# Residual rows of both mixers' ends formed by two row instructions instead of eight channel pieces turned back

## The chip, the cores and the metric

The kernel runs on one core of one Trainium2 chip. The metric is the device time of one execution, in microseconds (us). The engines that compute are TensorE (PE; its weight loads are listed apart as PEld), VectorE (DVE), ScalarE (ACT) and GpSimd (POOL); SyncE (SP) issues most of the DMAs.

## The reference, cut to what matters

The program is a trunk of two layers over 256 context tokens and 512 latent tokens of width 1024. Each layer is a sequence mixer (a linear recurrence, LRU, in layer 0; RWKV in layer 1), then a layer norm, then a mixture of 64 experts with 8 chosen for each token and one shared expert. What the change touches is what stands between mixer and experts:

```python
h = _layer_norm(DEEPNORM_ALPHA * h + m[2] * y, post_ln_g[i, 0], post_ln_b[i, 0])
u = _modulate(h, m[3], m[4])            # u = h * (1 + m[4]) + m[3]
y = _moe_ffn(u, router, bias, w_gu, w_down, sh_gu, sh_down)
h = _layer_norm(DEEPNORM_ALPHA * h + m[5] * y, post_ln_g[i, 1], post_ln_b[i, 1])
```

So each token needs two things at the end of a mixer: `u`, which the router and the experts read, and `h`, the residual, which is read again only behind the experts. Layer 0 has all 768 tokens here (6 tiles of 128), layer 1 only the 512 latent ones (4 tiles).

## The kernel before, in words

The stages follow one another: LRU mixer (to about 340 us), its end (340 to 478), the choice of experts, the sort and the experts of layer 0 (to about 1400), RWKV mixer (to about 2500), its end (to 2581), the experts of layer 1 (to about 3345) and the last norm. Products in fp32 are made from pieces split in two, three matmuls each. Inside the experts' loops the order of instructions is written by hand; everywhere else, the mixers' ends among it, a list scheduler of the compiler orders them, and each engine then runs its own list in that order.

A mixer's end is driven by `outputs` (L423). For each tile `t` it runs `gemm(t)`, the mixer's output product, and steps a generator `res(t, ...)` of `mixer_res` (L1911) from `yield` to `yield`, so that the steps of neighbouring tiles lie between each other. The steps of one tile:

- load the residual row tile `hin` (3 buffers in layer 0, 4 in layer 1); `post_ln` or `norm` (L400 to L421) leaves in it the normed rows, without the norm's gain and bias;
- turn it: eight 128x128 transposes on PE put the tile with channels on the partitions into `rt_px` (L1955). `rt_px` is 4 KB per partition in PSUM and has one buffer; whoever wants it next waits until its readers are done;
- form `uT`, the experts' input with channels on the partitions: eight pieces, each one instruction with a scale and a bias per channel (`mbc`, in which gain and modulation are folded together). Pieces with k in `UD` (1, 3, 5, 7) go to DVE (L1962), the others to ACT (L1964);
- form `hT`, the finished residual with channels on the partitions, in the same way with `mbx`: odd pieces on ACT (L1969), even ones on DVE (L1971);
- `route` (L685 to L717): eight matmuls of `uT` with the router's weights into `rt_pr`, a tanh on ACT (L687), and some twenty small DVE instructions; L712 writes `Mt`, the chosen experts, L717 `Wt`, their weights;
- turn `uT` back into rows (eight transposes into `rt_px`, L1977, and two copies on ACT, L1979) and send the rows to DRAM as `u_d` (L1984, on SP);
- turn `hT` back in the same way (again `rt_px`, again L1977 and L1979) and send the rows as `hm_d` (L1987, on POOL).

So `rt_px` is filled three times for a tile. When the last tile's product has been issued, the shared expert's weights are loaded into the mixer's freed memory (`ew`), split on ACT, DVE and POOL, and some of the shared expert's matmuls (`ph`, `py`, L95) are put among the steps of the tiles. When every tile's `Mt` is there, the sort begins on PE with `cc` (L793); the experts' weight loads follow behind it.

Of the kernel before, what the change touches and what calls it, by code (L numbers as in the profile page):

```python
# [9 lines left out]
F32 = mybir.dt.float32  # L10
# [3 lines left out]
AF = mybir.ActivationFunctionType  # L14
OP = mybir.AluOpType
# [4 lines left out]
D = 1024  # L20
KD = D // 128
# [6 lines left out]
NE = 64  # L28
# [243 lines left out]
class Kern:  # L272
# [181 lines left out]
    def lru(self, before, prepare, res, early):  # L454
        nc, ins, tc = self.nc, self.ins, self.tc
        with ExitStack() as st:
# [88 lines left out]

            S = {}

            def p0(j):
# [13 lines left out]
                for s, t0, n in SEGS:  # L562
# [3 lines left out]
                    for a in range(1, 4):  # L566
                        nc.vector.scalar_tensor_tensor(x, z[:, o + a:o + a + n], cw[:, a, j:j + 1], x, op0=OP.mult, op1=OP.add)
                S[j] = {"xc": xc}

# [187 lines left out]
    def moe(self, i, T, caps, u_d, acc_d, C, early, wst, late):  # L757
# [4 lines left out]
        nc, ins, tc = self.nc, self.ins, self.tc  # L762
# [3 lines left out]
        with ExitStack() as st:  # L766
            cq = st.enter_context(self.pool(name=f"moe_c{i}", bufs=1))
            wk = st.enter_context(self.pool(name=f"moe_k{i}", bufs=2))
# [12 lines left out]
            elist, ov, nov, novi = row("elist", 64, I32, 1), row("ov", 64, F32, 1), row("nov", 1, F32, 1), row("novi", 1, I32, 1)  # L781
# [190 lines left out]
            with tc.manual_schedule():  # L972
# [19 lines left out]
                for n in range(NB + 2):  # L992
# [40 lines left out]
                    elif n >= 2:  # L1033
                        nc.gpsimd.indirect_dma_start(out=acc_d[n % 2], out_offset=bass.IndirectOffsetOnAxis(ap=ix, axis=0),  # L1034
                                                     in_=yt[:C], in_offset=None, compute_op=OP.add)
                    if n == NB - 1:
                        late(lambda t, s: E.wp.tile(s, F32, name=f"late_{t}", tag=t, bufs=E.BW[t]))


            nr = nc.values_load(novi[0:1, 0:1], min_val=0, max_val=NE)  # L1040
            with tc.For_i(0, nr, 1) as it:
                e = nc.sync.value_load(olist[0:1, 1, bass.ds(it, 1)], min_val=0, max_val=NE - 1)
                p = nc.vector.value_load(olist[0:1, 0, bass.ds(it, 1)], min_val=0, max_val=NE - 1)
# [832 lines left out]
ES = ((2, 4, 2, 4), (2, 1, 4, 1))  # L1876
HB = (3, 4)
UB = (3, 4)
UD = ((1, 3, 5, 7), (1, 3, 5, 7))
VB = 5  # L1880
BUF = {'X1': 2, 'X2': 2, 'NN': 4, 'no': 2, 'ZT': 8, 'SU': 2, 'O': 2}

# [8 lines left out]
def trunk(tc, ins, out):  # L1891
    K = Kern(tc, ins, out)
    nc = tc.nc

    with ExitStack() as st:
# [12 lines left out]
        def stream(i, t):  # L1908
            return CTX if i == 0 and t < 2 else LAT

        def mixer_res(i):  # L1911
            P = {}

            def prepare(pool, psr):
                S = (CTX, LAT) if i == 0 else (LAT,)
                if i:
                    P["z1"] = K.ln_params(pool, 0, 1)
                for s in S:
                    if i == 0:
                        P[2, s] = pool.tile([128, D], F32, name=f"mb{s}")  # L1920
                        K.bcast_row(P[2, s], i, s, 2)

                    r = pool.tile([4 * KD, 128], F32, name=f"mbr{s}")
                    for n, x in enumerate((ins["post_ln_g"][i, 0], ins["post_ln_b"][i, 0], K.m_d[i][s, 4 * D:5 * D], K.m_d[i][s, 3 * D:4 * D])):
                        K.load(r[n * KD:(n + 1) * KD], x.rearrange("(k p) -> k p", p=128))
                    ps = psr.tile([128, 4, KD], F32, name="mb_ps", tag="rt_pr")
                    nc.tensor.transpose(ps.rearrange("p n k -> p (n k)"), r, K.ident[:4 * KD, :4 * KD])
                    x = pool.tile([128, 4, KD], F32, name=f"mbx{s}")
                    nc.vector.tensor_copy(x, ps)
                    P["x", s] = x  # L1930
                    c = P["c", s] = pool.tile([128, 2, KD], F32, name=f"mbc{s}")
                    nc.vector.scalar_tensor_tensor(c[:, 0], x[:, 2], 1.0, x[:, 0], op0=OP.add, op1=OP.mult)
                    nc.vector.scalar_tensor_tensor(c[:, 1], x[:, 2], 1.0, x[:, 1], op0=OP.add, op1=OP.mult)
                    nc.vector.tensor_tensor(c[:, 1], c[:, 1], x[:, 3], op=OP.add)

            def res(t, ys, wk, psr):
                s = stream(i, t)
                h = wk.tile([128, D], F32, name="hin", bufs=HB[i])
# [14 lines left out]
                px = psr.tile([128, KD, 128], F32, name="rt_px")  # L1953
# [6 lines left out]
                for k in range(KD):  # L1960
                    if k in UD[i]:
                        nc.vector.tensor_scalar(uT[:, k], px[:, k], c[:, 0, k:k + 1], c[:, 1, k:k + 1], op0=OP.mult, op1=OP.add)  # L1962
                    else:
                        nc.scalar.activation(uT[:, k], px[:, k], AF.Identity, scale=c[:, 0, k:k + 1], bias=c[:, 1, k:k + 1])  # L1964
                x = P["x", s]
                hT = wk.tile([128, KD, 128], F32, name="rt_hT", bufs=1)
                for k in range(KD):
                    if k % 2:
                        nc.scalar.activation(hT[:, k], px[:, k], AF.Identity, scale=x[:, 0, k:k + 1], bias=x[:, 1, k:k + 1])  # L1969
                    else:  # L1970
                        nc.vector.tensor_scalar(hT[:, k], px[:, k], x[:, 0, k:k + 1], x[:, 1, k:k + 1], op0=OP.mult, op1=OP.add)  # L1971

                def back(xT, y):

                    px = psr.tile([128, KD, 128], F32, name="rt_px")
                    for k in range(KD):
                        nc.tensor.transpose(px[:, k, :], xT[:, k], K.ident)  # L1977
                    for k in range(0, KD, 4):
                        nc.scalar.activation(y[:, k * 128:k * 128 + 512].rearrange("p (k d) -> p k d", k=4), px[:, k:k + 4, :], AF.Copy)  # L1979
# [3 lines left out]
                back(uT, u)  # L1983
                nc.sync.dma_start(u_d[i][t * 128:(t + 1) * 128, :], u)  # L1984
                yield
                back(hT, h)
                nc.gpsimd.dma_start(hm_d[i][t * 128:(t + 1) * 128, :], h)  # L1987
            return prepare, res

# [70 lines left out]
        fs, f = right()  # L2060
# [17 lines left out]
        P = {}  # L2078
        K.rwkv(first, done, begin, res)
        with P["rs"]:  # L2080
# [3 lines left out]
            with wst:  # L2084
                fs, f = right()
# [49 lines left out]
```

## Time and profile before

| what | time |
|---|---|
| median of 3 runs (3382.0 to 3406.42) | 3397.05 us |
| profiled execution | 3397.3 us |
| its span in the trace | 3395.5 us |
| PE busy in the span | 2976.2 us (88%) |
| DVE busy | 2403.6 us (71%) |
| ACT busy | 2006.7 us (59%) |
| POOL busy | 1125.8 us (33%) |
| mean granted TensorE clock, share of full speed | 0.878 |

An execution is one core's, so the time is that of this core. Busy shares over the whole span mix stages with different limits; the rows below are taken from the stretches that the change touches. A line of a timeline is one instruction, or several alike in a row ("x8"): its start, its time, the engine, the source line, what it writes and reads, and in brackets how long the engine stood idle before it and what ended that.

### The profile page before, as it was taken

Reading aid. Unit: us, or ns where it says so; the run is one execution under the profiler, and the core shown is the slowest. Engines: PE = TensorE matmul, PEld = TensorE weight load, DVE = VectorE, ACT = ScalarE, POOL = GpSimd, SP = SyncE. Lnnn points to the kernel's source line nnn. Section 1 sums busy time; section 2 is a strip of 40 time slices with the busy share of each in tenths; the row PEclk is TensorE's granted clock in tenths of the full one; section 3 lists DMA queues with packets and bytes.
Section 4 is the critical chain, followed back from the end, with each engine's and each line's share of the span. In section 5 each row is a group of like instructions: output and inputs, shape, how many; then the busy total and the mean of one; then the engine's idle time right before and its main releaser. Section 6 shows DMA issues by size and latency. Waiting matters only on the chain. (4 is left out here: it accounts for less than half of the span.)

```text
span 3395.5 us, 52648 instructions
## 1 busy us (share of the span) xinstructions
PE 2976.2 (88%) x17929; PEld 2076.3 (61%) x17929; DVE 2403.6 (71%) x4728; ACT 2006.7 (59%) x3835; POOL 1125.8 (33%) x1341
## 2 busy tenths in 40 slices
PE   7998768899999998498989998999877898899993
PEld 3665756667676665376757776767655665555551
DVE  4555557788878887767774756765554888789886
ACT  2664335667766776666645454654333676677773
POOL 0323002333333433122544455543421232333331
PEclk9998879999999999699975678577977999899997
DMA  6446339999999998433675666566524999999995
GB/s 218 126 133 195 116 147 271 307 318 333 339 292 322 330 314 283 137 105 125 152 192 147 176 186 184 147 185 169 171 97 172 320 327 330 309 353 356 344 341 175
DMA packets 329665, 784.71 MB, mean 231 GB/s; under 512 B 129176, under 2 KB 194008, under 8 KB 279856
## 3 DMA queue, kind: packets, MB, share of 16 engines
q1 hardware_dynamic: 276576, 668.36, 59.5%
q0 software_dynamic: 52816, 112.93, 13.9%
q8 instruction: 145, 2.38, 0.3%
q14 instruction: 128, 1.05, 0.1%
HBM read 644.66 MB, written 134.82 MB: 230 GB/s over the span
## 5 line engine op out<-in xcount | busy, mean ns | idle before, releaser
L95 PE MATMUL ph<-w1s,xs 128*128 128x512 f32 (+21 forms) x3216 | 808.1, 401 | 5.6 <-ACT xs L305 2.7
L308 DVE TENSOR_TENSOR w1s<-w,w1s 128x1024 fp32r<-128x1024 f32 x516 | 609.1, 1221 | 67.5 <-ACT w1s L305 66.7
L95 PEld LDWEIGHTS ph<-w1s,xs 128*128 128x128 f32 (+21 forms) x3216 | 490.6, 157 | 247.3 <-DVE xs L308 13.1
L1034 POOL DMA_INDIRECT acc_d<-yt,ix x150 | 303.9, 2026 | 949.3 <-ACT yt L141 312.5
L305 ACT ACTIVATE w1s<-w 128x1024 fp32r<-128x1024 f32 x516 | 516.8, 1057 | 5.3 <-DMA w<-in_moe_w_gu_dram 4.9
L95 PE MATMUL py<-w2s,hT 128*128 128x512 f32 (+22 forms) x1608 | 428.6, 417 | 38.4 <-DVE yt L138 25.5
L95 PEld LDWEIGHTS py<-w2s,hT 128*128 128x128 f32 (+22 forms) x1608 | 250.5, 163 | 160.4 <-issue 34.1
L305 ACT ACTIVATE xs<-px 128x512 fp32r<-128x512 f32 (+23 forms) x287 | 131.2, 457 | 358.8 <-DVE xs L308 224.8
L308 DVE TENSOR_TENSOR w2s<-w,w2s 128x1024 fp32r<-128x1024 f32 x258 | 303.6, 1217 | 8.1 <-ACT w2s L305 8.1
L305 ACT ACTIVATE w2s<-w 128x1024 fp32r<-128x1024 f32 x258 | 258.3, 1053 | 13.2 <-DMA w<-in_moe_w_down_dram 13.1
L308 DVE TENSOR_TENSOR xs<-px,xs 128x512 fp32r<-128x512 f32 (+23 forms) x287 | 146.4, 510 | 157.3 <-ACT xs L305 157.3
L932 POOL DMA_INDIRECT xg<-u_d,ix x150 | 215.8, 1438 | 89.1 <-issue 42.2
L141 ACT ACTIVATE yt<-py 128x512 f32<-128x512 f32 (+20 forms) x282 | 151.6, 593 | 45.6 <-PE py L95 25.7
L73 PE MATMUL px<-ident,xg 128*128 128x128 f32 (+25 forms) x1224 | 129.6, 249 | 44.8 <-DMA xg<-u_d,ix 44.8
L73 PEld LDWEIGHTS px<-ident,xg 128*128 128x128 f32 (+25 forms) x1224 | 111.2, 144 | 68.8 <-issue 61.0
L1690 POOL TENSOR_TENSOR SU<-SU,pC 64x128 f32<-64x128 f32 x176 | 96.6, 554 | 154.2 <-DVE SU L1710 130.9
L542 PE MATMUL in_ps<-uT,w_in 128*128 128x256 f32 (+1 forms) x768 | 143.3, 344 | 4.1 <-ACT w_in L305 2.1
L1189 PE MATMUL pt_ps<-xm,rw 128*128 128x256 f32 (+1 forms) x600 | 130.0, 370 | 14.3 <-ACT xm L305 7.9
L542 PEld LDWEIGHTS in_ps<-uT,w_in 128*128 128x128 f32 x768 | 118.6, 189 | 35.1 <-ACT w_in L305 6.4
L1535 PE MATMUL sc_ps<-X,uBK 64*128 64x128 f32 (+1 forms) x768 | 133.6, 358 | 0.7 <-POOL upt L1494 0.6
L1189 PEld LDWEIGHTS pt_ps<-xm,rw 128*128 128x128 f32 x600 | 102.1, 192 | 45.4 <-ACT xm L305 9.2
L1535 PEld LDWEIGHTS sc_ps<-X,uBK 64*128 64x128 f32 x768 | 113.3, 253 | 21.1 <-issue 8.4
(461 smaller groups left out, 5578.0 us busy)
## 6 DMA issues: line engine op xcount, KB each, us to landing
w<-in_moe_w_gu_dram SPq DMA_DIRECT2D x256, 1024.0 KB
w<-in_moe_w_down_dram SPq DMA_DIRECT2D x128, 1024.0 KB
ada_w<-in_ada_w_dram SPq DMA_DIRECT2D x96, 512.0 KB
O<-op SPq DMA_DIRECT2D x32, 768.0 KB
op<-NN SPq DMA_DIRECT2D x48, 256.0 KB
op<-NN SPq DMA_DIRECT2D x32, 384.0 KB
SU<-v_d SPq DMA_DIRECT2D x48, 256.0 KB
acc_d<-zrow SPq DMA_DIRECT2D x17, 512.0 KB
```

Of the source, the lines that this page charges most:

```text
L73: self.nc.tensor.transpose(px[:, k, :C], x[:C, k * 128:(k + 1) * 128], self.K.ident[:C, :C])
L95: self.nc.tensor.matmul(out[:C], x[a][:, :C], w[b], start=(first and a + b == 0), stop=(last and a == 1))
L141: self.nc.scalar.activation(yt[:C, c * 512:(c + 1) * 512], py[:C, c, :], AF.Copy)
L305: nc.scalar.activation(hi, src, AF.Copy)
L308: (lo_eng or nc.vector).tensor_tensor(lo, src, hi.bitcast(F32), op=OP.subtract)
L542: nc.tensor.matmul(ps[:, s, :n], whl[a][:, k, :], uT[b][:, k, t0:t0 + n], start=(k == 0 and a == 0 and b == 0), stop=(k == KD - 1 and a == 1))
L932: nc.gpsimd.indirect_dma_start(out=x[:C], out_offset=None, in_=u_d, in_offset=bass.IndirectOffsetOnAxis(ap=IW[blk][0], axis=0))
L1034: nc.gpsimd.indirect_dma_start(out=acc_d[n % 2], out_offset=bass.IndirectOffsetOnAxis(ap=ix, axis=0), in_=yt[:C], in_offset=None, compute_ ...
L1189: nc.tensor.matmul(ps[:, s, :n], w[a][:, k, :], x[k][b][:, s0:s0 + n], start=(k == 0 and a == 0 and b == 0), stop=(k == KD - 1 and a == 1))
L1535: nc.tensor.matmul(sc[h][:, c, :nr, :], BK[r64(h), c].rearrange("p a t -> p (a t)"), X[r64(h), :, c, :], start=True, stop=True)
L1690: nc.gpsimd.tensor_tensor(SV[z, g2][r64(0), :, k2], S[r64(0), :, k], P[z, g]["pC"][:, k].to_broadcast([64, 2, 64]), op=OP.mult)
```

## The change

Four things are changed, all but the last in `mixer_res`:

- The eight `hT` pieces, the eight transposes that turn them back and the two ACT copies behind these are gone. In their place two DVE instructions multiply the row tile `hin` by the gain and add the bias, in place and over all 1024 channels at once; they stand behind the sending of `u_d`. `hm_d` is sent as before.
- For that `prepare` loads two more tiles per mixer, the rows `post_ln_g` and `post_ln_b` spread over 128 partitions (512 KB each). In layer 1, the corresponding rows of the experts' norm of layer 0 get names of their own.
- `UD` is empty: all eight `uT` pieces are made on ACT.
- In the experts' function, the load of the number of overflow blocks (`nr`) into the engines' registers is moved from behind the hand-ordered part to its last step, ahead of the `late` tiles.

```diff
@@ -1034,10 +1034,10 @@
                     if n == NB - 1:
+                        nr = nc.values_load(novi[0:1, 0:1], min_val=0, max_val=NE)
                         late(lambda t, s: E.wp.tile(s, F32, name=f"late_{t}", tag=t, bufs=E.BW[t]))
 
 
-            nr = nc.values_load(novi[0:1, 0:1], min_val=0, max_val=NE)
             with tc.For_i(0, nr, 1) as it:
@@ -1876,7 +1876,7 @@
-UD = ((1, 3, 5, 7), (1, 3, 5, 7))
+UD = ((), ())
@@ -1913,8 +1913,13 @@
             def prepare(pool, psr):
                 S = (CTX, LAT) if i == 0 else (LAT,)
+                P["ln"] = K.ln_params(pool, i, 0)
                 if i:
-                    P["z1"] = K.ln_params(pool, 0, 1)
+                    P["z1"] = []
+                    for n in ("post_ln_g", "post_ln_b"):
+                        x = pool.tile([128, D], F32, name=f"z1_{n}")
+                        K.load(x, ins[n][0, 1:2, :].to_broadcast([128, D]))
+                        P["z1"].append(x)
@@ -1927,7 +1932,6 @@
-                    P["x", s] = x
@@ -1962,14 +1966,6 @@
-                x = P["x", s]
-                hT = wk.tile([128, KD, 128], F32, name="rt_hT", bufs=1)
-                for k in range(KD):
-                    if k % 2:
-                        nc.scalar.activation(hT[:, k], px[:, k], AF.Identity, scale=x[:, 0, k:k + 1], bias=x[:, 1, k:k + 1])
-                    else:
-                        nc.vector.tensor_scalar(hT[:, k], px[:, k], x[:, 0, k:k + 1], x[:, 1, k:k + 1], op0=OP.mult, op1=OP.add)
@@ -1983,7 +1979,8 @@
                 back(uT, u)
                 nc.sync.dma_start(u_d[i][t * 128:(t + 1) * 128, :], u)
                 yield
-                back(hT, h)
+                for x, op in zip(P["ln"], (OP.mult, OP.add)):
+                    nc.vector.tensor_tensor(h, h, x, op=op)
                 nc.gpsimd.dma_start(hm_d[i][t * 128:(t + 1) * 128, :], h)
```

The scheduler makes new lists from this. Three places of them are shown, by the program's order alone. First PE at the end of the RWKV mixer, from the end of the last product (L1863) on; before:

```order
L1863 MATMUL ro_ps<-hin,alpha_i 128x512 x2
L1977 MATMUL rt_px<-ident,rt_uT 128x128 x8
L1977 MATMUL rt_px<-ident,rt_hT 128x128 x8
L1955 MATMUL rt_px<-ident,hin 128x128 x8
L95 MATMUL ph<-ew_26112,xs_26210 128x512
```

and in the changed kernel (L1959 and L1973 are L1955 and L1977 of before; `ph` is the shared expert):

```order
L1863 MATMUL ro_ps<-hin,alpha_i 128x512 x2
L1959 MATMUL rt_px<-ident,hin 128x128 x8
L685 MATMUL rt_pr<-rw,rt_uT 128x64 x8
L1973 MATMUL rt_px<-ident,rt_uT 128x128 x8
L1959 MATMUL rt_px<-ident,hin 128x128 x8
L95 MATMUL ph<-ew_25985,xs_26065 128x512
```

Before, the first tile is still to be turned back twice when the last product ends, and the second is then turned. Now the first is finished ahead of the last product, the second tile's three steps follow it, and the third tile is turned before the shared expert's matmuls. Behind them stand, before, three tiles' route and six groups of L1977, and now two tiles' route and two groups of L1973.

Second, DVE at the last tile of the same stretch; before, from the end of the third tile's route to the start of the last one's:

```order
L717 TENSOR_SCALAR Wt<-rt_sc,rt_ws 128x64
L1962 TENSOR_SCALAR rt_uT<-rt_px,mbc_25722 128x128 x3
L308 TENSOR_TENSOR xs_26474<-rt_uT,xs_26473 128x512
L1962 TENSOR_SCALAR rt_uT<-rt_px,mbc_25722 128x128
L1971 TENSOR_SCALAR rt_hT<-rt_px,mbx_25720 128x128
L308 TENSOR_TENSOR xs_26474<-rt_uT,xs_26473 128x512
L1971 TENSOR_SCALAR rt_hT<-rt_px,mbx_25720 128x128
L688 TENSOR_SCALAR rt_sc<-rt_sc 128x64
```

and in the changed kernel (L308 are second halves of splits for the shared expert, L115 is its gating):

```order
L717 TENSOR_SCALAR Wt<-rt_sc,rt_ws 128x64
L1983 TENSOR_TENSOR hin<-hin,post_ln_g 128x1024
L1983 TENSOR_TENSOR hin<-hin,post_ln_b 128x1024
L308 TENSOR_TENSOR hT_26206<-pt,hT_26205 128x256
L115 TENSOR_TENSOR sg<-sg,ph 128x256
L308 TENSOR_TENSOR xs_26311<-rt_uT,xs_26310 128x512 x2
L688 TENSOR_SCALAR rt_sc<-rt_sc 128x64
```

The pieces have left DVE's list, and the two row instructions stand between one tile's route and the next one's.

Third, SP ahead of the end of the LRU mixer, one piece of the difference (`zrow` fills buffers in DRAM with zeros, 512 KB each; `mb` and `mbr` are what `post_ln` and `mbc` need):

```order
 L299 DMA w_out<-in_lru_w_out_dram 128x8x128 x8
-L299 DMA mb_2324<-m_d_68 128x1024
-L299 DMA mbr_2326<-in_post_ln_g_dram 8x128
+L299 DMA post_ln_g<-in_post_ln_g_dram 128x1024
+L299 DMA post_ln_b<-in_post_ln_b_dram 128x1024
 L299 DMA u_d_73<-zrow 256x1x512
 L299 DMA acc_d_75<-zrow 256x1x512
```

The two new loads take the place of `mb` and of the first quarter of `mbr`, which now come behind the zero fills.

## Rows read from the trace of the kernel before

**Rows 1.** Windows: stretch, length, busy time per engine, TensorE clock, DMA share
```profile
core 0: us, PE busy (x) PEld busy (x) DVE busy (x) ACT busy (x) POOL busy (x), PEclk, DMA share, GB/s
...
349.20:406.20 57.00, 56.93 (x368) 51.85 (x368) 30.84 (x139) 17.94 (x31) 0.61 (x1) 0.95 0.15 48
406.20:478.50 72.30, 44.98 (x196) 36.39 (x197) 45.31 (x184) 36.39 (x68) 9.22 (x7) 0.67 0.30 109
...
2506.80:2581.00 74.20, 60.73 (x275) 47.26 (x276) 40.62 (x179) 35.00 (x69) 6.91 (x6) 0.80 0.14 57
```

**Rows 2.** Timeline, last tile of the LRU mixer's end, from turning to sort
```profile
463.08 1.10 PE L1955 MATMUL rt_px<-ident,hin 128*128 128x128 f32 x8 [1.18 <-ACT hin L1979]
464.21 0.46 ACT L1964 ACTIVATE rt_uT<-rt_px,mbc 128x128 f32<-128x128 f32 x1 [1.19 <-PE rt_px L1955]
...
465.15 0.46 ACT L1964 ACTIVATE rt_uT<-rt_px,mbc 128x128 f32<-128x128 f32 x1 [0.48 <-DVE rt_uT L1962]
...
468.16 0.69 PE L685 MATMUL rt_pr<-rw,rt_uT 128*128 128x64 f32 x2 [0.19 <-DVE rt_uT L1962]
...
469.74 0.18 DVE L688 TENSOR_SCALAR rt_sc<-rt_sc 128x64 f32<-128x64 f32 x1
...
472.25 1.97 PE L1977 MATMUL rt_px<-ident,rt_uT 128*128 128x128 f32 x8 [3.40 <-ACT rt_hT L1969]
474.05 0.20 DVE L712 CAST Mt<-rt_rp 128x64 bf16<-128x64 f32 x1
474.25 1.09 ACT L1979 ACTIVATE um<-rt_px 128x512 f32<-128x512 f32 x2 [2.06 <-PE rt_px L1977]
...
475.39 1.97 PE L1977 MATMUL rt_px<-ident,rt_hT 128*128 128x128 f32 x8 [1.18 <-ACT um L1979]
...
478.54 0.48 PE L793 MATMUL cc<-ones_b,Mt 128*64 128x64 bf16 x6 [1.17 <-ACT hin L1979]
```

**Rows 3.** Timeline: the last product's end, and the turning before that of rows 2
```profile
404.82 1.31 PE L653 MATMUL o_ps<-wx,yT 128*128 128x256 f32 x9
...
448.81 1.09 PE L1955 MATMUL rt_px<-ident,hin 128*128 128x128 f32 x8 [1.18 <-ACT hin L1979]
```

**Rows 4.** Timeline: first loads of the shared expert's weights, and its first matmuls
```profile
402.42 8.91 SPq L299 DMA_DIRECT2D ew<-in_moe_sh_gu_dram  x4
...
436.50 7.71 PE L95 MATMUL ph<-ew,xs 128*128 128x512 f32 x24 [1.46 <-DVE hin L403]
```

**Rows 5.** Timeline, end of the RWKV mixer: the last turning and the sort
```profile
2565.86 1.97 PE L1955 MATMUL rt_px<-ident,hin 128*128 128x128 f32 x8 [1.18 <-ACT hin L1979]
...
2580.95 0.42 PE L793 MATMUL cc<-ones_b,Mt 128*64 128x64 bf16 x4
```

**Rows 6.** Timeline, start of the RWKV mixer: eight scaled pieces on ACT alone
```profile
1402.68 2.91 ACT L1130 ACTIVATE u<-u_ps,cs 128x128 f32<-128x128 f32 x8 [2.06 <-PE u_ps L1128]
```

**Rows 7.** Durations by line, row instructions on DVE: ns least/median/most
```profile
L1944 DVE TENSOR_TENSOR hin<-hin,post_ln_g x4: 1209/1210/1212, 2456.6 to 2462.8; 128x1024 f32<-128x1024 f32 x4
```

**Rows 8.** Timeline before the LRU mixer's end: zero fills, then the first norm
```profile
323.95 14.54 SPq L299 DMA_DIRECT2D acc_d<-zrow  x11
...
347.82 1.28 DVE L403 SCALAR_TENSOR_TENSOR hin<-hin,o_ps 128x512 f32<-128x512 f32 x2 [1.41 <-DMA hin<-in_ctx_dram]
```

**Rows 9.** Timeline: a small DVE instruction beside a split on POOL
```profile
421.33 2.35 POOL L308 TENSOR_TENSOR ew<-ew,ew 128x1024 fp32r<-128x1024 f32 x1 [2.75 <-ACT ew L305]
421.38 2.37 DVE L701 TENSOR_TENSOR rt_g<-rt_g,t 128x64 f32<-128x64 f32 x1
```

**Rows 10.** Timeline on SP: first weight loads of the experts, behind each sort
```profile
487.28 0.96 SPq L299 DMA_DIRECT2D w<-in_moe_w_gu_dram  x2
...
2590.98 0.95 SPq L299 DMA_DIRECT2D w<-in_moe_w_gu_dram  x2
```

**Rows 11.** Chain that ended last: behind the register loads of the second layer
```profile
3345.71 3.45 DMA acc_d<-yt,ix
```

**Rows 12.** Windows, one stretch of the RWKV mixer's main loop
```profile
1700.00:2000.00 300.00, 278.79 (x2220) 205.79 (x2218) 192.91 (x493) 155.76 (x471) 138.62 (x290) 0.65 0.66 169
```

## The prediction

> **What bounds the kernel now.** I read the windows of the two stretches first [rows 1]. While the LRU mixer's last products run (349 to 406 us), PE is busy for 56.9 of 57.0 us: nothing there is gained by relieving another engine. From 406 to 478 it is busy for only 45.0 of 72.3 us, and DVE (45.3) and ACT (36.4) are not full either. At the RWKV mixer's end PE is busy for 60.7 of 74.2 us, DVE for 40.6. So in both tails the engines wait for each other, and 27 and 13 us of PE's time are idle.
>
> For what, the timeline of a last tile shows [rows 2]. The turning of the tile at 463.08 starts 1.18 us behind an ACT copy of the tile before: it had to wait until `rt_px` was emptied. Then the tile fills that buffer three times one after the other: turned at 463.08; uT's and hT's sixteen pieces read it until shortly before 472.25, where PE has idled 3.40 us for `rt_hT`; uT turned back and copied; hT turned back from 475.39 and copied; and only then the sort's first matmul at 478.54, with ACT's copy as its releaser. `Mt`, which the sort needs, was there at 474.25 (474.05 + 0.20). Four microseconds of the last tile are thus hT's alone, and the whole cycle, from the turning at 448.81 [rows 3] to that at 463.08, is 14.3 us, of which PE's transposes are a small part. The RWKV mixer's last cycle has 15.1 us (2565.86 to 2580.95) [rows 5]. The chain through the single buffer `rt_px` sets both tails.
>
> What follows moves with the tails: the experts' first weight loads are issued 8.7 us behind the first sort and 10.0 us behind the second [rows 2, 5, 10]. A sort that starts earlier lets the loads start earlier, so I let a gain there count in full.
>
> **What the change removes, adds and moves.** *hT.* A tile loses a fill of `rt_px`: eight transposes (1.09 us [rows 3] to 1.97 us [rows 2], by the clock), two ACT copies (1.09 us [rows 2]) and two hops of 1.18 us between them. It loses the eight hT pieces as well, which stand in rows 2 between uT's end (the last router matmul at 468.16) and 472.25, some 4 us. Together 4 + 1.5 + 1.1 + 2.4 = 9 us of the cycle of 14.3. `rt_px` is then held for turning 1.1, uT pieces about 3, turning back 1.1, copies 1.1 and some 2 us of hops: about 8 us.
>
> *Row instructions.* Two per tile on DVE. The same shape on the same tile, L1944, takes 1.21 us [rows 7], so 2.4 us a tile, against eight DVE pieces (four of uT, four of hT) of about the 0.46 us of ACT's, or 3.7 us, that leave. DVE loses work. The row instructions wait for nothing new but the turning, nothing on PE reads them, and the order puts them between one tile's route and the next one's; what can stand behind them is the next `Mt`, by at most 2.4 us. I charge nothing in the sum, since PE has the shared expert's matmuls meanwhile, and 2.4 us for each tail's last tile in the upper bound.
>
> *uT on ACT alone.* Now ACT's pieces of 0.46 us have 0.48 us of idle between them, waiting for DVE's [rows 2]: the two engines take turns, and eight pieces need about 3.9 us (464.21 to 468.16). The nearest case of eight on ACT alone is L1130, 2.91 us [rows 6]. From both sides: 2.9 (back to back) to 3.7 (8 x 0.46); I take 3, for L1130 too reads PSUM with a scale. So about 1 us less for each of ten tiles.
>
> [...]
>
> *Loads.* Two rows of 512 KB per mixer. For the RWKV mixer they fall where the DMA share is low (0.14 in the tail [rows 1]); no cost. For the LRU mixer, SP's order puts `mb` and `mbr` behind the twelve zero fills, whose last eleven take 14.54 us from 323.95 on [rows 8]; what follows them on that queue is the tiles' loads, and the first norm instruction waits for one (347.82, 1.41 us [rows 8]). Two more loads of 1.3 us each (14.54 / 11 by row 8) shift them: 2.6 us late, call it 3, between 0 (if the loads fit beside) and 5.
>
> *Registers.* The moved `nr` load: the chain behind the old place still waits 3.45 us for `acc_d` [rows 11], so an earlier register load is hidden. I take 0 (0 to 2 gained).
>
> **The sum.** *LRU's end.* PE's work from 349.2 to the sort is 56.9 + 45.0 = 101.9 us [rows 1]. Six groups of hT transposes leave, 6 x 1.09 to 6 x 1.97, about 8: 94 us remain at the same clocks. Were PE never idle behind a start 3 us later, the sort would start at 349.2 + 3 + 94 = 446. Not all waits go. The last tile still has turning 1.1 to 2.0, uT 3, the last router matmul, and DVE's route (469.74 to 474.25, 4.5 us [rows 2]) behind one another: 10 to 11 us, some 5 of which PE idles. The shared expert's weights also set a bound: first loads at 402.42, 3.7 us before the last product's end at 406.13 (404.82 + 1.31), first matmuls at 436.50 [rows 3, 4]. So I add 7: the sort at 453 instead of 478.5, **25 us less**. Bounds: 446 (no idle time) and 462 (as many idle microseconds as 16 of the 27 now), or 17 to 32.
>
> *RWKV's end.* 60.7 us of PE's work [rows 1], less four groups (4.4 to 7.9, say 6): 54.7 from 2506.8 on is 2561.5. The shared expert's `py` matmuls now stand between the last turning back and the sort and cover most of the last route; 1.5 us of wait is left. The sort at 2563 instead of 2581, **18 us less**; bounds 2558 and 2570, or 11 to 23.
>
> Together 43 us of the profiled execution's 3397.3, which equals the median of the runs (3397.05) within 0.3: **3354 us**. TensorE's clock is no term: it was granted at 0.67 in the LRU tail with its idle time and at 0.95 ahead of it [rows 1], so a denser tail could only add to the gain, and the bounds at no idle time take in some of that.
>
> **The rivals.**
> *Half only.* The chain moves to DVE or to the shared expert. DVE has 76 us of work in the 129 us of LRU's end [rows 1], and its list is in order: a route that waits holds the norm of a later tile behind it. The `ew` splits can also hold `ph`, and with it the last tile, since the last product's end does not come earlier (PE was full until 406). Then only the last tile's 9 us and one or two cycles' part are won at each end: about 13 + 10, **3374**. For it: 34 us lie between `ew`'s first load and `ph` [rows 4]. Against it: `ph` waited for a `hin` instruction of DVE there, not for the splits.
>
> A split on POOL of 2.35 us beside a small DVE instruction that took 2.37 us [rows 9] shows a further way: row instructions that stand still beside POOL's splits. There are three POOL splits in a tail, each up to 2.4 us: at most 7 us per end, so 14 in all, **3368** if all hit; I put it into this rival, not into the sum. [...]
>
> *Hidden anyway.* The tails are held by PE's other work, the gain stays at the last tile's two copies and transposes: 4 us at each end, **3389**. Against it: 27 and 13 us of idle PE.
>
> *Slower.* The new lists are made by a scheduler that sees the whole program, and it has moved instructions in the RWKV mixer's main loop too, though the change touches nothing there. The loop has a PE busy for 279 of 300 us [rows 12], so it has at most 7% of idle time to give back, but a worse order can add waits without such a bound. From 43 us more in that loop on (4% of the 1100 us between the first experts' end and the second sort) the whole is not faster: **3397 or more**, say 3410. Against it: the same dependences and the same scheduler; I expect plus or minus 10 us of it, and the range takes that in.
>
> *No effect of the row edit* (the scheduler delays hT's substitutes to where they hold `hin` and so the next load): the LRU end has three `hin` buffers; the order shows the rows of each tile ahead of the next route, which excludes it but for a few microseconds.
>
> **How the numbers follow.** Chances: forecast 0.70 (both tails shortened, its own range 3397.3 - 55 to 3397.3 - 28, so 3342 to 3369, with the loop's 10 us 3332 to 3379), half only 0.14, hidden 0.06, slower 0.06, and 0.04 for a gain well beyond (the clock comes up in the tail and the last products end as before). The range from 3328 to 3382 leaves out hidden, slower and a part of the last, and the rim of the forecast: about 2 in 10. One per cent, about what a measurement of this kernel can tell from no change, is 34 us: faster means below 3363. Of the forecast's 0.70 some 0.56 lie there, and of the other cases 0.06; slower than 3431 takes 0.03, half of the slower case; the rest is within 1%.
>
> **What would show it.** In the changed profile: no transposes of `rt_hT`; turnings at LRU's end 7 to 10 us apart where only the buffer held them; uT's eight pieces on ACT within 3 us; the two row instructions at 1.2 us each; the first sort near 453 and the second about 43 us earlier than 2581, at 2538; first norm instruction about 3 us later than 347.8; the time from sort to the last instruction unchanged in both layers. It would be wrong if PE's idle time in the tails stayed, if a DVE wait stood ahead of the last `Mt`, or if the stretch between the first experts' end and the RWKV mixer's end changed by more than 10 us.

## The result and the profile after

The changed kernel takes 3338.44 us (median of 4 runs, 3329.78 to 3359.48), the kernel before 3390.99 us beside it (4 runs, 3382.0 to 3406.42). The ratio is 0.9846 with a 95% interval of 0.9811 to 0.9881, so 40 to 64 us less. Forecast were 3354 us and 43 us less, with a range of 3328 to 3382. The profiled execution of the changed kernel has a span of 3328.0 us (before: 3395.5), at a mean granted clock of 0.887 (before: 0.878).

Two changed kernels of the same text can differ by more than a stage's gain (see `after_again`), so the parts below are told from fixed places of the program to fixed places, not from the span's start. From the first zero fill (`u_d<-zrow` on SP) to the first routed expert's matmul it is 190.3 us before and 157.4 after (33 less). From the first turning of the RWKV mixer's end to the first routed expert's matmul of layer 1 it is 114.6 us before and 86.4 after (28 less). Together 61 us less. The experts themselves take the same: 774.1 and 773.7 us from that matmul to the span's end.

The two ends in windows of the changed kernel, to the first matmul of the sort; columns as in [rows 1]. The first window begins at the same time of the trace as there, which is 4.0 us ahead of the end's first output product here (353.20 us) and at that product before (349.16 us):

```profile
core 0: us, PE busy (x) PEld busy (x) DVE busy (x) ACT busy (x) POOL busy (x), PEclk, DMA share, GB/s
349.20:443.50 94.30, 83.59 (x519) 74.28 (x520) 75.03 (x285) 44.06 (x87) 11.31 (x9) 0.90 0.37 129
2467.90:2517.80 49.90, 48.17 (x242) 38.14 (x242) 38.53 (x147) 28.25 (x61) 7.92 (x6) 0.92 0.20 80
```

PE was busy for 101.9 of 129.3 us and for 60.7 of 74.2 us [rows 1]; now it is for 83.6 of 94.3 and for 48.2 of 49.9. Taken from the first output product on (353.20 to 443.46), LRU's end has PE busy for 83.3 of 90.3 us. So in RWKV's end 1.7 us of idle time are left of 13, and in LRU's end 7 of 27. The third thing to see is the clock: 0.95 and 0.67 in the two parts of LRU's end and 0.80 in RWKV's [rows 1], now 0.92 (from the first product on) and 0.92.

The last tile of LRU's end, the answer to [rows 2], and the sort behind it (timeline; start, time, engine, line, what, and the idle time before with what ended it):

```profile
434.07 1.09 PE L1959 MATMUL rt_px<-ident,hin 128*128 128x128 f32 x8 [0.95 <-ACT hin L421]
...
436.56 2.90 ACT L1968 ACTIVATE rt_uT<-rt_px,mbc 128x128 f32<-128x128 f32 x8
...
437.69 1.21 DVE L1983 TENSOR_TENSOR hin<-hin,post_ln_g 128x1024 f32<-128x1024 f32 x1
438.93 1.23 DVE L1983 TENSOR_TENSOR hin<-hin,post_ln_b 128x1024 f32<-128x1024 f32 x1
...
440.38 1.92 PE L1973 MATMUL rt_px<-ident,rt_uT 128*128 128x128 f32 x8
...
441.28 0.19 DVE L688 TENSOR_SCALAR rt_sc<-rt_sc 128x64 f32<-128x64 f32 x1
...
443.46 0.43 PE L793 MATMUL cc<-ones_b,Mt 128*64 128x64 bf16 x5 [1.17 <-ACT um L1975]
...
445.09 0.20 DVE L712 CAST Mt<-rt_rp 128x64 bf16<-128x64 f32 x1
...
445.34 0.26 PE L793 MATMUL cc<-ones_b,Mt 128*64 128x64 bf16 x1 [1.45 <-DVE Mt L712]
```

The turning no longer waits for a copy out of `rt_px`: its releaser is the norm of its own tile (L421). The eight uT pieces are one run on ACT of 2.90 us. The row instructions take 1.2 us each. And the sort's last matmul now waits for the last tile's `Mt` (L712), where before `Mt` had been there for 4 us. The wait at the end has changed its kind: from the buffer to the choice of experts itself.

RWKV's end, the answer to [rows 5]: two turnings, the shared expert's second product, and the sort.

```profile
2485.89 1.04 PE L1959 MATMUL rt_px<-ident,hin 128*128 128x128 f32 x8
...
2492.42 1.87 PE L1959 MATMUL rt_px<-ident,hin 128*128 128x128 f32 x8 [1.18 <-ACT um L1975]
...
2514.92 3.00 PE L95 MATMUL py<-ew,hT 128*128 128x512 f32 x12
2517.84 0.28 PE L793 MATMUL cc<-ones_b,Mt 128*64 128x64 bf16 x3
2518.65 0.22 PE L793 MATMUL cc<-ones_b,Mt 128*64 128x64 bf16 x1 [0.52 <-DVE Mt L712]
```

Two turnings stand 6.5 us apart where only the buffer held the second (its releaser is the copy of uT's rows, L1975), where 7 to 10 were expected of LRU's end, and the `py` matmuls cover the last route but for 0.52 us.

What waited for whom in LRU's tail: the view of waits, before (406 to 479 us; total, times, longest):

```profile
DVE rt_uT L1962 <- ACT rt_uT L1964: 14.0, 12, 4.5
...
PE rt_px L1977 <- ACT rt_hT L1969: 9.7, 2, 6.3
...
PE rt_px L1955 <- ACT hin L1979: 6.4, 3, 4.0
...
PE rt_px L1977 <- ACT um L1979: 5.0, 4, 1.5
```

and after (406 to 446 us):

```profile
PE rt_pr L685 <- ACT rt_uT L1968: 2.7, 2, 1.9
...
PE ph L95 <- DVE ew L308: 2.1, 1, 2.1
```

21 us of PE's waiting for `rt_px` to be filled from or emptied by hT's and uT's steps have gone. What is left, besides the waits at the sort shown above, are the pieces of uT themselves and, new, the split of the shared expert's weights.

Last, the start of LRU's end on SP and DVE, the answer to [rows 8]:

```profile
324.98 15.30 SPq L299 DMA_DIRECT2D acc_d<-zrow  x11
340.33 1.31 SPq L299 DMA_DIRECT2D mb<-m_d  x1
...
351.86 1.28 DVE L403 SCALAR_TENSOR_TENSOR hin<-hin,o_ps 128x512 f32<-128x512 f32 x2 [1.07 <-DMA hin<-in_ctx_dram]
```

From the first zero fill to this norm instruction it is 27.5 us (324.37 to 351.86), against 24.5 before (323.33 to 347.82): the 3 us of the forecast.

### The profile page after: what moved, and what is told of

Its sections match the earlier page's. It is cut to its first block, busy times and chain, and to the rows that moved or that the text cites. A ratio compares the mean times of both kernels' runs of the same rounds, so it can differ in the third digit from the quotient of the medians.

```text
span 3328.0 us, 52403 instructions
## 1 busy us (share of the span) xinstructions
PE 2926.6 (88%) x17849; PEld 2041.4 (61%) x17849; DVE 2389.7 (72%) x4668; ACT 1986.2 (60%) x3815; POOL 1120.3 (34%) x1341
## 5 line engine op out<-in xcount | busy, mean ns | idle before, releaser
L308 DVE TENSOR_TENSOR w1s<-w,w1s 128x1024 fp32r<-128x1024 f32 x516 | 609.2, 1222 | 65.2 <-ACT w1s L305 62.9
L308 DVE TENSOR_TENSOR w2s<-w,w2s 128x1024 fp32r<-128x1024 f32 x258 | 303.7, 1218 | 8.7 <-ACT w2s L305 8.6
L308 DVE TENSOR_TENSOR xs<-px,xs 128x512 fp32r<-128x512 f32 (+23 forms) x287 | 146.4, 510 | 157.6 <-ACT xs L305 150.8
L1690 POOL TENSOR_TENSOR SU<-SU,pC 64x128 f32<-64x128 f32 x176 | 87.6, 502 | 160.0 <-DVE SU L1710 139.5
L1710 DVE TENSOR_TENSOR SU<-SU,pg 64x128 f32<-64x128 f32 x176 | 48.2, 275 | 120.9 <-PE pg L1708 97.2
```

The costliest lines, as they stand in the source:

```text
L308: (lo_eng or nc.vector).tensor_tensor(lo, src, hi.bitcast(F32), op=OP.subtract)
L1690: nc.gpsimd.tensor_tensor(SV[z, g2][r64(0), :, k2], S[r64(0), :, k], P[z, g]["pC"][:, k].to_broadcast([64, 2, 64]), op=OP.mult)
L1710: nc.vector.tensor_tensor(S, S, pg[:, 2], op=OP.add)
```

## The experiments

All stages in one table; each from one profile. A: first zero fill to the first routed expert's matmul. B: first turning of RWKV's end to the first routed expert's matmul of layer 1. C: the RWKV mixer, from its first scaled pieces (L1130) to the first turning of its end. Ratios are to the kernel before, in runs beside it on the same chip.

| kernel | A | B | A + B | C | ratio and interval |
|---|---|---|---|---|---|
| before | 190.3 | 114.6 | 304.9 | 1130.3 | |
| changed | 157.4 | 86.4 | 243.8 | 1123.8 | 0.9846 (0.9811 to 0.9881) |
| after_again | 157.6 | 86.5 | 244.1 | 1139.2 | 0.9817 (0.9737 to 0.9896) |
| after_third | 155.2 | 84.8 | 240.0 | 1108.7 | 0.9829 (0.9779 to 0.9878) |
| rows_only | 161.1 | 98.0 | 259.1 | 1130.2 | 0.9838 (0.9770 to 0.9906) |
| uact_only | 192.3 | 109.8 | 302.1 | 1153.5 | 1.0015 (0.9983 to 1.0047) |
| before_halves | 159.7 | 96.9 | 256.6 | 1134.3 | 0.9836 (0.9792 to 0.9880) |
| ln_late | 156.9 | 84.5 | 241.4 | 1141.9 | 0.9844 (0.9782 to 0.9907) |
| rows_pool | 163.2 | 93.9 | 257.1 | 1144.5 | 0.9892 (0.9829 to 0.9956) |
| after_halves | 156.7 | 83.0 | 239.7 | 1121.4 | 0.9792 (0.9729 to 0.9855) |
| after_later | 153.9 | 84.8 | 238.7 | 1132.5 | 0.9817 (0.9769 to 0.9865) |
| halves_later | 153.1 | 82.9 | 236.0 | 1128.4 | 0.9786 (0.9724 to 0.9847) |
| halves_later_again | 155.2 | 82.4 | 237.6 | 1125.7 | 0.9764 (0.9706 to 0.9822) |

**How steady a profile is.** `after_again` and `after_third` are the changed kernel itself.

> The changed kernel itself once more. It tells how far one profile's stages differ from another's of the same kernel: theory (the RWKV mixer's stretch between the first experts' end and its own end varies with the granted clock from run to run, the ends do not): LRU's end (first turning to first sort) within 1 us of 79.6, RWKV's end within 1.5 us of 50.0, the stretch between 1344.1 and 2467.9 (1123.8 us) off by 5 to 20 us. Rival (the stretch is fixed by the order): it too within 3 us.

> The changed kernel a third time, on one chip with the next two, as the measure for them: by the two profiles so far, LRU's end 79.6 us, RWKV's 50.0; the stretch of the RWKV mixer between them 1120 to 1140 us, and with it the time 3325 to 3345.

A and B of the three profiles agree within 2.4 and 1.7 us. C does not: 1108.7, 1123.8 and 1139.2 us, of one and the same instruction list. Over the 14 runs of this kernel the time goes with the mean granted clock: 3308.45 us at 0.890, 3336 in the middle at about 0.881, 3359.48 at 0.872. So the theory holds: C differs from run to run and the ends hardly do. The mean granted clock of the three profiled executions was 0.892, 0.887 and 0.881 in the same order, and within C of the middle one it was 0.77. The third profile's C lies below the 1120 to 1140 us expected of it. It also means that C says nothing on the order that the scheduler gave the RWKV mixer, and that the whole time of a few runs tells two kernels apart only from some 15 us on; for less, A and B have to do.

**The row instructions alone.**

```diff
 UB = (3, 4)
-UD = ((), ())
+UD = ((1, 3, 5, 7), (1, 3, 5, 7))
```

> The changed kernel with UD as before, so uT's pieces alternate between DVE and ACT again, and the residual rows stay row instructions. Theory (three fills of the one rt_px buffer set both tails, and taking one fill and the hT pieces away is the change): most of the gain stays, first sort 28 to 33 us and second 45 to 55 us earlier than before, the time 40 to 50 us under before's; a turning holds rt_px about 1 us longer per tile than in the changed kernel. Rival (the pieces of uT that wait for each other were the cost): under 15 us of gain.

3348.57 us, a ratio of 0.9838, 45 us under the kernel before, as expected. A and B are 46 us shorter than before's; the moved uT pieces are worth the other 15 (244 against 259). The rival, that the pieces waiting for each other were the cost, falls: without their alternation's end most of the gain is there.

**uT on ACT alone.** The same edit to the kernel before.

```diff
-UD = ((1, 3, 5, 7), (1, 3, 5, 7))
+UD = ((), ())
```

> The kernel before with UD empty alone, hT's pieces and their turning back kept. Theory (fills): uT's eight pieces take 3 us instead of 3.9, so 1 us for each of ten tiles where the chain through rt_px sets the tail, 5 to 10 us of gain. Rival (uT's alternation was the cost): over 30 us. Second rival (VectorE is the better engine for these): 0 or slower.

A ratio of 1.0015 (0.9983 to 1.0047): nothing, so the 5 to 10 us expected didn't come; 0 is the second rival's number, though not for its reason. A is 2.0 us longer and B 4.8 shorter. The pieces themselves did what was expected, but the next ones took it back. The timeline of its last tile in LRU's end:

```profile
468.76 2.90 ACT L1964 ACTIVATE rt_uT<-rt_px,mbc 128x128 f32<-128x128 f32 x8 [1.19 <-PE rt_px L1955]
...
471.69 0.41 DVE L1971 TENSOR_SCALAR rt_hT<-rt_px,mbx 128x128 f32<-128x128 f32 x1 [6.74 <-ACT rt_uT L1964]
...
476.25 1.97 PE L1977 MATMUL rt_px<-ident,rt_uT 128*128 128x128 f32 x8 [4.11 <-ACT rt_hT L1969]
```

uT's eight pieces take 2.90 us instead of 3.9, DVE stands idle for 6.74 us meanwhile, and then hT's pieces alternate as before, now with two splits for the shared expert and the route among them; PE waits 4.11 us for `rt_hT`, where it was 3.40 [rows 2]. So this edit is worth nothing by itself and 15 us in the ends behind the other one. Eight pieces on ACT were better than four on each engine as soon as hT's pieces were gone (259.1 to 243.8), and the choice hardly mattered before (304.9 to 302.1); eight on DVE alone were not run.

**The buffer alone.** The kernel before with `rt_px` in two halves of 2 KB per partition each, nothing removed:

```diff
-                px = psr.tile([128, KD, 128], F32, name="rt_px")
+                ph = [psr.tile([128, 4, 128], F32, name="rt_px", bufs=2) for _ in range(2)]
+                px = [ph[k // 4][:, k % 4] for k in range(KD)]
...
-                    px = psr.tile([128, KD, 128], F32, name="rt_px")
-                    for k in range(KD):
-                        nc.tensor.transpose(px[:, k, :], xT[:, k], K.ident)
                     for k in range(0, KD, 4):
+                        px = psr.tile([128, 4, 128], F32, name="rt_px", bufs=2)
+                        for j in range(4):
+                            nc.tensor.transpose(px[:, j, :], xT[:, k + j], K.ident)
...
```

> The kernel before with rt_px cut into two halves of four channel blocks, each a buffer of its own in the same PSUM memory: a fill of the second half can start while the first is still read, and the other way round; all pieces, transposes and copies stay. Theory (the wait for the whole buffer to be emptied sets the tails): 10 to 25 us of gain, in both tails. Rival (the pieces and copies on DVE and ACT set them by their own work, whatever the buffer): within 5 us of before.

3341.65 us, a ratio of 0.9836: twice the upper end of the expected gain, and as much as the whole change brings within the intervals. All pieces, all transposes and all copies are still there. PE's waits in LRU's tail (405 to 447 us, the whole list; before, 21 us of them were for the filling and emptying of `rt_px`):

```profile
PE rt_px L1979 <- ACT rt_hT L1970: 2.8, 2, 1.6
PE rt_pr L685 <- DVE rt_uT L1963: 1.7, 3, 0.9
PE rt_px L1979 <- ACT um L1980: 1.1, 1, 1.1
PE ph L95 <- ACT xs L305: 0.8, 1, 0.8
PE cc L793 <- ACT hin L1980: 0.7, 1, 0.7
PE ph L95 <- ACT ew L305: 0.6, 1, 0.6
```

Of the 21 us, 3.9 are left. So it was the one whole buffer that the tails waited for, and the work of the pieces and copies that fill and empty it is not the bound. One thing changed with the cut: the scheduler made new lists from it, in which, for example, uT of RWKV's first tile is turned back ahead of the last product and not behind it. What such an order would bring with a whole buffer was not tried. The windows over the two ends (to the sort's first matmul):

```profile
349.20:446.70 97.50, 89.44 (x563) 78.12 (x562) 73.42 (x319) 54.11 (x99) 10.01 (x8) 0.92 0.30 107
2476.00:2534.90 58.90, 54.96 (x274) 42.58 (x274) 38.10 (x171) 34.81 (x70) 6.96 (x6) 0.91 0.16 65
```

The first of them begins 1.1 us behind the first output product (348.12). From the same product and the same turning to the sort, both kernels have 838 PE instructions, and yet PE is busy for 145.5 us here and for 162.7 before: the same work, 17 us less, at a clock of 0.92 and 0.91 where the ends before had 0.95, 0.67 and 0.80. What the clock does to a row can be read within the trace of the kernel before. Two of the router's matmuls take 0.33 us where the granted clock was 1.00 (363.89 to 364.22), and 0.69 in the tail [rows 2], where it was 0.50 (468.16 to 468.85). Eight transposes take 1.09 us at 1.00 (from 448.81 on [rows 3]) and 1.97 at 0.50 (from 472.25 on [rows 2]). The first pair of matmuls:

```profile
363.89 0.33 PE L685 MATMUL rt_pr<-rw,rt_uT 128*128 128x64 f32 x2
```

The faster work is a second part of the gain, which no term of the forecast had; the rest is idle time.

**The same cut in the changed kernel.**

> The changed kernel with rt_px cut into two halves as in before_halves. Theory (rt_px no longer sets the tails in the changed kernel: PE is busy for 48.4 of 50.6 us in RWKV's end, DVE for 34.7 of 37.3 at the end of LRU's): under 8 us of gain in all, far below the 52 us that the same cut gave the kernel before. Rival (two fills of one buffer still set them): 15 to 25 us more.

3320.58 us, 0.9792. A and B are 4 us shorter than in two profiles of the changed kernel and as long as in the third (239.7 against 243.8, 244.1 and 240.0), so between nothing and 4: in the ends the expectation holds, and `rt_px` sets the changed kernel's ends hardly any more. The whole time fell by more. It is 20.6 us under the changed kernel on the same chip (3341.18), which is the rival's 15 to 25. The ends don't account for that. C is 17.8 us shorter than in that kernel's profile beside it, but the changed kernel's own profiles differ by 30.5 us there, so where the rest comes from is open.

**Where the new rows are loaded.** First behind `mb` and `mbr`, in `prepare`:

```diff
-                P["ln"] = K.ln_params(pool, i, 0)
                 if i:
...
                     nc.vector.tensor_tensor(c[:, 1], c[:, 1], x[:, 3], op=OP.add)
+                P["ln"] = K.ln_params(pool, i, 0)
```

> The changed kernel with its two new row loads issued behind mb and mbr instead of ahead of them; nothing else. Theory: in the changed kernel SP issues mb at 340.3 behind the zero fills, and DVE's first norm instruction waits for it until 347.7; with mb ahead of the fills again the LRU mixer's end starts 3 to 4 us earlier, and since PE is nearly full from there on, the first sort is 2 to 4 us earlier than 443.5 and the time as much less than the changed kernel's. Rival: the start is hidden by other waits, 0.

The expectation failed: the time is the changed kernel's, and the first norm comes later still, 29.3 us behind the first zero fill instead of 27.5.

```profile
354.97 1.28 DVE L403 SCALAR_TENSOR_TENSOR hin<-hin,o_ps 128x512 f32<-128x512 f32 x2 [6.33 <-DMA hin<-in_ctx_dram]
```

`mb` came early again, but the two rows now stand directly ahead of `hin` on SP, and the norm waits 6.33 us for that. It needs both; the rows belong behind both. So the next one loads them behind the third tile's `hin` (layer 1: the first's):

```diff
-                P["ln"] = K.ln_params(pool, i, 0)
+                P["ln"] = [pool.tile([128, D], F32, name=n, bufs=1) for n in ("post_ln_g", "post_ln_b")]
...
                     K.hin[t] = h
+                if t == (2 if i == 0 else 0):
+                    for n, x in zip(("post_ln_g", "post_ln_b"), P["ln"]):
+                        K.load(x, ins[n][i, 0:1, :].to_broadcast([128, D]))
                 yield
```

> The changed kernel with only the move of the two new row loads behind the first tiles' loads, rt_px whole. Theory (ln_late gained nothing since the row loads still stood ahead of hin on SP): the first turning comes at 358 to 360 instead of 364, first sort at 437 to 439; 5 to 6 us under the changed kernel in its LRU end, nothing in the RWKV end. Rival (the LRU end is bound behind its start): first sort within 2 us of 443.5.

The first norm comes 24.4 us behind the first zero fill, as before the change, and A is 153.9 against 157.4, 157.6 and 155.2: 1 to 4 us, less than the 5 to 6 expected. In the whole time it can't be told (3329.32 beside 3329.72 us of the changed kernel on the same chip).

**The row instructions on POOL.**

```diff
-                    nc.vector.tensor_tensor(h, h, x, op=op)
+                    nc.gpsimd.tensor_tensor(h, h, x, op=op)
```

> The changed kernel with its two row instructions per tile on POOL instead of DVE. Theory (in the changed kernel DVE sets the LRU mixer's tail: 34.7 of 37.3 us busy there): 2.4 us per tile leave DVE, the first sort is 4 to 8 us earlier than 443.5, RWKV's end hardly changes (DVE 39 of 51 us). Rival (the row instructions lie beside waits; on POOL they take about 2.35 us each by the split's row and hold DVE's two-input instructions still meanwhile): the same or up to 6 us later.

Slower than the changed kernel: 3359.52 us, A + B 257.1, 13 more. The expected gain did not come. Two lines of LRU's end show a price, and three of RWKV's end where the sort waits:

```profile
419.57 2.37 POOL L1983 TENSOR_TENSOR hin<-hin,post_ln_b 128x1024 f32<-128x1024 f32 x1
419.57 2.41 DVE L712 CAST Mt<-rt_rp 128x64 bf16<-128x64 f32 x1
...
2540.92 2.98 PE L95 MATMUL py<-ew,hT 128*128 128x512 f32 x12
2543.74 1.89 PE L685 MATMUL rt_pr<-rw,rt_uT 128*128 128x64 f32 x16
...
2551.32 0.26 PE L793 MATMUL cc<-ones_b,Mt 128*64 128x64 bf16 x1 [4.60 <-DVE Mt L712]
```

On POOL a row instruction takes 2.35 to 3.1 us, and a small DVE instruction beside it can take as long: this cast of 128x64 takes 0.20 us in the changed kernel (445.09). Instructions with two inputs, which the rival named, took longer too: two L308 splits of 128x512 took 3.00 us from 446.14 on, beside the row instruction of 445.63 (2.35 us), and 1.24 us from 430.52 on with POOL idle. So the edit took the row instructions off DVE and held other instructions of DVE up, and it doesn't settle whether DVE sets LRU's tail. In RWKV's end the sort now waits 4.60 us for the last `Mt`. A part of that is the new list: the `py` matmuls stand ahead of the last tile's router matmuls, while in the changed kernel they stand behind them (2514.92) and cover the last route. How much of the 13 us is the order was not measured.

**Both together.** `after_halves` with the rows loaded as in `after_later`, run on two chips:

> after_halves with the two new rows of each mixer loaded behind the first tiles' loads (layer 0: behind the third tile's hin; layer 1: behind the first), so that neither mb nor hin waits for them. Theory: the first turning of LRU's end comes 3 to 5 us earlier after the last product before it than in the changed kernel, first sort 3 to 5 us earlier; about 4 us under after_halves. Rival: the row loads then delay the first tiles' row instructions and with them the hin buffers, 0.

> halves_later again, beside the changed kernel on the same chip. By the stages of the first profiles it is 6 us shorter up to the first sort and 2.4 us in RWKV's end: 8 to 10 us under the changed kernel, 5 rounds may just tell it. Rival (the 16 us between the medians so far are real): 14 to 20 us under, with the difference in the RWKV mixer's stretch, by another order there.

3322.19 and 3315.86 us, ratios of 0.9786 and 0.9764 to the kernel before. A + B is 236.0 and 237.6, the shortest of all, 2 to 8 us under the changed kernel's three profiles. On the same chip, with six runs each, it is at 3315.86 (3287.51 to 3334.34) beside 3329.72 (3309.67 to 3349.43) of the changed kernel: the ends account for some 5 us of the 14, and where the rest comes from is as open as for `after_halves`. It is the fastest version found. Over all runs, the changed kernel's 14 have a median of 3336 us and the 14 of the versions with the buffer cut 3321, so the whole time is likely shorter by more than the ends are.

## Why the prediction was right, point by point

The direction, the mechanism and the range held; the size was too small, 43 us against 52 by the medians (40 to 64) and 61 in the two ends. That the time lies in the range is in part luck. From fixed places, the first sort comes 36 us earlier (155.2 us behind the first zero fill before, 119.1 after) against 25 and an upper bound of 32, and the second 24 (74.2 us behind the first turning before, 50.0 after) against 18 and an upper bound of 23. The measured 3338 us lies below the forecast's own 3342 and within the range only by the 10 us that were allowed for the RWKV mixer's loop.

**What bounds the kernel.** Right, and shown by `before_halves`: relief of the buffer, with all work kept, shortens A and B by 48 us, and PE's waits for it fall from 21 to 4 us in LRU's tail. The new order that came with it is the one thing that was not held fixed.

**hT's steps.** Right in kind. In the changed kernel a turning waits for its own tile's norm, or 1.18 us for uT's copy. `rows_only` gives the part: 46 us in the ends.

**Row instructions.** 1.17 to 1.23 us in nine of the ten tiles, as taken from L1944; nothing charged. In both last tiles they end before the route's first DVE instruction has its input or 0.4 us behind it, so the sum was right to leave them out. The rival of POOL's splits beside DVE did occur, on the row instructions of RWKV's first tile and on a small instruction of LRU's last norm. The changed kernel's timeline:

```profile
428.94 2.40 POOL L308 TENSOR_TENSOR ew<-ew,ew 128x1024 fp32r<-128x1024 f32 x1 [3.52 <-ACT ew L305]
429.03 2.33 DVE L326 SCALAR_TENSOR_TENSOR ln_rs<-rs_t,ln_rs 128x1 f32<-128x1 f32 x1
...
2468.83 5.69 POOL L308 TENSOR_TENSOR ew<-ew,ew 128x1024 fp32r<-128x1024 f32 x2 [4.83 <-ACT ew L305]
2469.94 2.33 DVE L1983 TENSOR_TENSOR hin<-hin,post_ln_g 128x1024 f32<-128x1024 f32 x1 [2.21 <-ACT hin L421]
2472.31 3.30 DVE L1983 TENSOR_TENSOR hin<-hin,post_ln_b 128x1024 f32<-128x1024 f32 x1
```

A DVE instruction on 128 single numbers takes 2.33 us beside a split on POOL (2.40), and 0.14 to 0.16 us five other times in this stretch (405 to 446 us); it belongs to the last tile's norm, for which the turning at 434.07 waits. Such a pair was in the kernel before too [rows 9], so it is no loss by the change. The two row instructions of RWKV's first tile took 5.6 us instead of 2.4, beside the two splits of 5.69. PE had no idle time meanwhile (from 2467.86 to 2486.9), so they cost nothing there.

**uT on ACT.** 2.90 us for eight was right (3 were taken). Its worth was put at 10 us for ten tiles whatever else is done. It was nothing alone, and 15 in the ends behind the row instructions: the two edits aren't additive, since without the row instructions hT's pieces held the same buffer next.

**Loads.** 3 us late, as forecast, and the cause was only half seen: `hin`, too, is late when the rows stand ahead of it (`ln_late`).

**Registers.** Nothing gained, as taken: between the last two scatters at the end of the experts of layer 1 it is 4.10 us before (3341.61 to 3345.71) and 4.12 after (3273.60 to 3277.72).

**The clock.** This is the step that failed: "TensorE's clock is no term". The forecast took PE's 101.9 and 60.7 us, subtracted 8 and 6 for the transposes and left the rest "at the same clocks", so 94 and 54.7. Measured from the first product and the first turning to the sort were 83.3 and 48.2. The transposes were sized right: the ten groups of hT take 14.25 us of PE's time (8.20 and 6.05) in the trace before, against the 14 taken. The remaining 17 us (94 + 54.7 - 131.5) are PE's other work, done faster as the granted clock rose from 0.67 to 0.88 in LRU's tail and from 0.80 to 0.92 in RWKV's end. The upper bound of the gain, "no idle time" at the old clocks, was therefore no bound. The same goes on behind the second sort: from the sort to the first routed expert's matmul it is 40.4 us before, at 0.75, and 36.5 after, at 0.90; the forecast let this stretch move unchanged. Behind the first sort it is 38.3 us instead of 35.1, as the sort now begins 1.9 us ahead of its last input, and at a clock of 0.81 instead of 0.89.

**The rivals.** "Half only" (3374) didn't happen: the gain was 40 to 64 us and not 23. Whether DVE's list would be the next bound isn't settled, since `rows_pool` held DVE up in another way. Of the rival's parts, `ew`'s splits did show, 2.1 us at one place. "Hidden anyway" falls with A and B. "Slower", by a worse order in the RWKV mixer: not seen; C of three profiles of the changed kernel lies on both sides of before's 1130.3. The range allowed 10 us for it, but the difference from run to run alone is 15 either way.

**The signs.** The first sort came at 443.5 instead of 453, the second at 2517.8 instead of 2538. Of the signs of being wrong, PE's idle time went (7 and 1.7 us are left). The sort does wait for DVE's last `Mt`, by 1.45 and 0.52 us. The RWKV mixer's stretch changed by 6.5 us in the first profile, but by 9 and 22 in the other two, so its limit of 10 us was narrower than the difference from run to run.

**What stays open.** How much of the clock's rise is due to the missing idle time and how much to which work stands next to which; no run varied that alone. That idle time by itself doesn't tell the clock can be seen in the RWKV mixer of the kernel before. The stretch just ahead of that of [rows 12], with the same columns:

```profile
1500.00:1700.00 200.00, 180.83 (x952) 138.30 (x951) 142.73 (x269) 130.56 (x304) 75.11 (x109) 0.96 0.49 133
```

PE is busy here for 90% at a clock of 0.96, and in [rows 12] for 93% at 0.65.

## What to carry to other kernels

Where engines wait for each other, look for the one buffer that is filled several times per tile, and count its fills: here either one fill less or two half buffers in the same memory took 46 to 48 us off the two ends, and the second fix on top of the whole change took 4 at most off them. When a denser order takes PE's idle time away, work out the gain's upper bound with PE's rows at the clock that the same kind of work shows ahead of the waits (0.95 here), since PE's busy time itself can shrink; the clock need not rise, as the mixer's stretch at 0.65 shows. An edit that speeds up one reader of a buffer can be worth nothing while another reader holds the buffer next, as it was here.

## What the runs showed of the hardware that was not expected

- As many and the same PE instructions in the two ends took 162.7 us at clocks of 0.79 and 0.80 (means over each end) and, in another order and with the buffer cut, 145.5 us at 0.92 and 0.91.
- One kernel's executions differed by 51 us (3308.45 to 3359.48), with the mean granted clock going from 0.890 to 0.872. Three of them were profiled, and there the difference lies in the RWKV mixer (1108.7 to 1139.2 us) and hardly in the ends (A + B 240.0 to 244.1).
- Two stretches of the RWKV mixer with PE busy for 90% and 93% were granted 0.96 and 0.65 [rows 12].
- A cast of 128x64, with one input where the expectation of `rows_pool` named instructions with two, took 2.41 us beside a row instruction of 2.37 us on POOL, and 0.20 us without one (445.09 in the changed kernel).
